# Causal attention whose value products run in two passes instead of three, with the rows' sums taken elementwise

## The chip, the cores and the metric

The kernel runs on one core of one Trainium2 chip. The metric is the device time of one execution in microseconds (us); less is better. The core has a matrix engine (PE, with a separate track PEld for loading the stationary operand), a vector engine (DVE), an activation engine (ACT), a general-purpose engine (POOL) and a queue engine that issues DMA transfers (SP). Each engine runs its own instructions strictly in the order in which they stand in its program, and waits at an instruction until the semaphores that this instruction names have come. PE writes to PSUM only; POOL reads and writes SBUF only.

## The reference, cut to what matters

The whole program is one decoder layer over 2048 tokens of width 1024: an RWKV-7 branch and a latent attention branch on one normalised input, gated and merged, then a mixture of experts. The change lies in the attention branch, 8 heads of 96-wide queries and keys and 64-wide values:

```python
s = (jnp.einsum('bqhd,bkhd->bhqk', q_nope[:, start:end], k_nope[:, :end])
     + jnp.einsum('bqhr,bkr->bhqk', q_rope[:, start:end], k_rope[:, :end]))
s = s.astype(jnp.float32) * scale
causal = jnp.arange(end)[None, :] <= jnp.arange(start, end)[:, None]
p = jax.nn.softmax(jnp.where(causal, s, -jnp.inf), axis=-1).astype(v.dtype)
outs.append(jnp.einsum('bhqk,bkhd->bqhd', p, v[:, :end]))
```

The softmax is done as usual in two steps: the numerator p = exp(s - max), the product of p with the values, and the sum of p over the keys of each query, by which the product is divided later.

## The kernel before, in words

The program goes through phases: input projections (`phase_a`), attention with the RWKV scan beside it (`phase_d`), merge, output projection and router (`phase_f`), experts (`phase_g`), final norm (`phase_z`). All matrix operands of `phase_d` that need accuracy are split into a high part, rounded to the matrix engine's fast 32-bit format (`F32R`), and a low part, the rest. `split` does this: ACT copies the high part (L143), and another engine, for attention POOL, subtracts it from the source for the low part (L144).

`phase_d` works through 32 units, one for each head `h` and each block `qb` of 512 queries. A unit has `4*qb + 4` steps, one for each tile of 128 keys (`kt`); the last four lie on the diagonal and are 512, 384, 256 and 128 queries wide. Over all units that makes 320 steps, 224 of them 512 wide and 32 of each narrower width. In `pass2` a step does this:

- PE makes the scores of 128 keys by up to 512 queries, keys on partitions, in three products (L1044 to L1046) and on the diagonal a fourth that adds the mask (L1048), into a PSUM tile `st` (2 buffers).
- ACT takes the exponential to SBUF, `pf` (L1052, 3 buffers), and copies its high part `ph` (L143). POOL subtracts for the low part `pl` (L144). These have 4 buffers each.
- Three steps later (`flush`), PE multiplies with the values. The value tile `av` holds for each key 192 columns: 64 of the values' low part, 64 of their high part and 64 ones. L1031 multiplies `ph` with [high, ones] (128 columns), L1032 multiplies `ph` with the low part into the same 64 rows of PSUM, and L1036 (for one step in each unit L1061, at the end) multiplies `pl` with [high, ones]. So rows 0 to 63 of `pv` collect the product and rows 64 to 127 the sum of p.
- At the end of a unit ACT copies the product `ob` (L1064) and one row of sums `lb` (L1065) to SBUF, and two DMAs store them.

Between the steps `other()` fills in the rest: `pass1` of a later unit, in which PE makes rough scores with queries on partitions (L982, tiles `sh`, 3 buffers), DVE reduces each to its maximum (L985, masked L988), and the negated maxima (L994) go through PE (L998) and ACT (L999) into a 97th row of the queries; and pieces of the RWKV scan (PE products `sx` on lines 852 to 880, DVE steps on lines 858 to 873, later `post`, lines 889 to 925). A scheduler of the framework then sets the final order of each engine's instructions from its own estimate of time and from the priorities of the code, so that instructions of neighbouring steps stand interleaved. Once per head `load_k` splits the next head's keys and values (POOL, `ak` and `av`).

Of the kernel before, what the change touches and what calls it, by code (L numbers as in the profile page):

```python
# [10 lines left out]
F32 = mybir.dt.float32  # L11
F32R = mybir.dt.float32r
# [3 lines left out]
AF = mybir.ActivationFunctionType  # L16
OP = mybir.AluOpType
# [5 lines left out]
NT = S // 128  # L23
# [64 lines left out]
class K:  # L88
# [842 lines left out]
    def d_open(self):  # L931

        self.dst = ExitStack()
        kp = self.kp = self.dst.enter_context(self.tc.tile_pool(name="attnkv", bufs=1, side="right",
                                                                reuse_waits="tile"))
        self.av = [kp.tile([128, NT, 192], F32R, name="av%d" % j) for j in range(2)]
        for t in self.av:
            self.nc.vector.tensor_copy(t[:, :, 128:], self.c["ones"][:, None, :64].to_broadcast([128, NT, 64]))
        self.idr = kp.tile([128, 128], F32R, name="identr")
        self.nc.vector.tensor_copy(self.idr, self.ident)  # L940
        self.cmq = kp.tile([128, 512], F32, name="cmq")
        self.dma(self.cmq, self.I["cmq"])
        self.q0 = self.load_q(0, 0)
        self.kv0 = self.load_k(0)
        self.p0 = self.pass1(kp, "rw", 4, self.kv0[0], self.q0, 0)
# [56 lines left out]
    def phase_d(self):  # L1002
        nc, tc = self.nc, self.tc
        V, A, T = nc.vector, nc.scalar, nc.tensor
        self.Od = [self.dram("Od%d" % q, [4, 128, 512]) for q in range(4)]
        self.Ld = [self.dram("Ld%d" % q, [H, 512]) for q in range(4)]
        with ExitStack() as st:
            st.push(self.dst.pop_all())
            self.psum(st, "d")
            ap = st.enter_context(tc.tile_pool(name="attn", bufs=1, side="right", reuse_waits="tile"))  # L1010
# [12 lines left out]
            def pass2(h, qb, kk, v, qq, other):  # L1023
                pv = self.pst("pv", 2)
                nk = 4 * qb + 4
                todo, keep = [], []

                def flush():
                    kt, j0, ph, pl = todo.pop(0)
                    cs = slice(j0 * 128, 512)  # L1030
                    T.matmul(pv[:, cs], v[:, kt, 64:], ph[:, cs], start=kt == 0, stop=False)  # L1031
                    T.matmul(pv[0:64, cs], v[:, kt, 0:64], ph[:, cs], start=False, stop=False)  # L1032
                    if kt == 4 * qb:
                        keep.append((kt, pl))
                    else:
                        T.matmul(pv[:, cs], v[:, kt, 64:], pl[:, cs], start=False, stop=False)  # L1036

                for kt in range(nk):
                    j0 = max(0, kt - 4 * qb)
                    cs = slice(j0 * 128, 512)  # L1040
                    ks = slice(kt * 128, (kt + 1) * 128)
                    ps = self.pst("st", 2)
                    dg = kt >= 4 * qb
                    T.matmul(ps[:, cs], kk[0][:, ks], qq[0][:, cs], start=True, stop=False)  # L1044
                    T.matmul(ps[:, cs], kk[0][:96, ks], qq[1][:96, cs], start=False, stop=False)
                    T.matmul(ps[:, cs], kk[1][:96, ks], qq[0][:96, cs], start=False, stop=not dg)  # L1046
                    if dg:
                        T.matmul(ps[:, j0 * 128:(j0 + 1) * 128], self.identb, self.cmkb, start=False, stop=True)  # L1048
                    pf = ap.tile([128, 512], F32, name="pf", bufs=3)
                    ph = ap.tile([128, 512], F32R, name="ph", bufs=4)  # L1050
                    pl = ap.tile([128, 512], F32R, name="pl", bufs=1 if kt == 4 * qb else 4, tag="plx" if kt == 4 * qb else "pl")
                    A.activation(pf[:, cs], ps[:, cs], AF.Exp, scale=SCALE)  # L1052
                    self.split(ph[:, cs], pl[:, cs], pf[:, cs], nc.gpsimd)
                    todo.append((kt, j0, ph, pl))
                    if len(todo) > 3:
                        flush()
                    other()
                while todo:
                    flush()
                kt, pl = keep[0]  # L1060
                T.matmul(pv, v[:, kt, 64:], pl, start=False, stop=True)  # L1061
                ob = ap.tile([64, 512], F32, name="ob", bufs=2)
                lb = ap.tile([1, 512], F32, name="lb", bufs=2)
                A.activation(ob, pv[0:64], AF.Copy)  # L1064
                A.activation(lb, pv[64:65], AF.Copy)  # L1065
                self.dma(self.Od[qb][h // 2, 64 * (h % 2):64 * (h % 2) + 64], ob)
                self.dma(self.Ld[qb][h:h + 1], lb)

            units = [(h, qb) for h in range(H) for qb in range(4)]
            steps = [4 * qb + 4 for h, qb in units]  # L1070
# [741 lines left out]
```

## Time and profile before

| | |
|---|---|
| time, median of 3 runs | 2710.17 us (2708.5 to 2712.07) |
| the profiled execution's own time | 2706.18 us |
| its span, first to last instruction | 2704.4 us |
| attention stage (1065 to 1732 us of the span) | 667 us |
| PE busy in the stage | 634.23 us |
| ACT busy in the stage | 462.57 us |
| DVE busy in the stage | 442.38 us |
| POOL busy in the stage | 415.51 us |
| TensorE clock granted, mean over the stage | 0.96 of full speed |

How to read the profile: it is one execution, taken by the hardware profiler. Busy time of an engine is the time in which at least one of its instructions was recorded as running; an instruction that has started and is held up inside the chip counts as busy. Matmuls are pipelined, so that the recorded length of one is longer than its distance to the next. A wait is idle time of an engine, put down to the instruction whose semaphore came last. Times of day are counted from the first instruction. The attention stage is here the stretch from the first value product (at 1066.6 us) to the last one (at 1731.7 us), widened to whole numbers.

### The profile page before, as it was taken

How to read it: one execution, taken by the hardware profiler on the slowest of the kernel's cores; microseconds unless marked ns; L12 is line 12 of the kernel's file. 1: busy time of each engine (PE TensorE's matmuls, PEld its weight loads, DVE VectorE, ACT ScalarE, POOL GpSimd, SP SyncE). 2: the span in 40 equal slices, each digit the busy share in tenths (PEclk: the TensorE clock that was granted, in tenths of full speed). 3: DMA queues.
4: the chain of work that ended last, by engine and by line, in shares of the span. 5: the costliest groups of instructions: out<-in, count | busy, mean ns of one | idle time of the engine just before them, and what ended most of it. 6: DMA issues, size and time to landing. Idle time of an engine off the chain costs nothing. (4 is left out here: it accounts for less than half of the span.)

```text
span 2704.4 us, 42459 instructions
## 1 busy us (share of the span) xinstructions
PE 2493.0 (92%) x14868; PEld 2033.2 (75%) x14868; DVE 1957.0 (72%) x3466; ACT 1424.3 (53%) x2539; POOL 961.8 (36%) x676
## 2 busy tenths in 40 slices
PE   8999999999999998989999999999999878999991
PEld 6777778788787886767777777777888667989880
DVE  8766699777748994676666766666666678888883
ACT  6554243465443423666776767632232246878774
POOL 3111612401112222556665665402012145555540
PEclk9999999999999998999999999999999979999995
DMA  4556444435563435444443441674554377999987
GB/s 147 125 146 172 137 140 134 171 102 133 142 177 105 138 122 173 129 122 133 129 123 95 129 129 41 205 225 137 184 167 148 125 228 235 329 288 318 299 246 264
DMA packets 334443, 452.46 MB, mean 167 GB/s; under 512 B 170320, under 2 KB 216272, under 8 KB 332944
## 3 DMA queue, kind: packets, MB, share of 16 engines
q1 hardware_dynamic: 320656, 416.03, 49.3%
q0 software_dynamic: 13568, 33.67, 5.5%
q8 instruction: 118, 1.93, 0.3%
q14 instruction: 101, 0.83, 0.1%
HBM read 318.06 MB, written 138.33 MB: 169 GB/s over the span
## 5 line engine op out<-in xcount | busy, mean ns | idle before, releaser
L151 PE MATMUL am<-h,aw 128*128 128x512 f32 x1104 | 440.8, 400 | 21.2 <-ACT h L237 8.5
L144 POOL TENSOR_TENSOR pl<-pf,ph 128x512 fp32r<-128x512 f32 (+1 forms) x320 | 372.8, 1181 | 238.5 <-ACT ph L143 163.3
L153 PE MATMUL am<-h,aw 128*128 128x512 f32 x1104 | 437.8, 397 | 11.9 <-POOL aw L144 7.5
L152 PE MATMUL am<-h,aw 128*128 128x512 f32 x1104 | 437.3, 396 | 0.1
L1562 PE MATMUL gg<-hh,gu 128*128 128x256 f32 (+5 forms) x1024 | 271.0, 338 | 5.4 <-DVE hh L144 5.0
L151 PEld LDWEIGHTS am<-h,aw 128*128 128x128 f32 x1104 | 210.8, 191 | 70.1 <-ACT h L237 8.5
L153 PEld LDWEIGHTS am<-h,aw 128*128 128x128 f32 x1104 | 210.3, 191 | 60.3 <-POOL aw L144 8.7
L1563 PE MATMUL gg<-hh,gu 128*128 128x128 f32 (+5 forms) x1024 | 249.2, 250 | 0.0
L152 PEld LDWEIGHTS am<-h,aw 128*128 128x128 f32 x1104 | 210.5, 191 | 48.6 <-DVE h L238 2.4
L1052 ACT ACTIVATE pf<-st 128x512 f32<-128x512 f32 (+1 forms) x320 | 167.6, 529 | 119.2 <-PE st L1046 65.2
L1562 PEld LDWEIGHTS gg<-hh,gu 128*128 128x128 f32 x1024 | 195.8, 191 | 13.1 <-DVE hh L144 6.6
L1563 PEld LDWEIGHTS gg<-hh,gu 128*128 128x128 f32 x1024 | 198.6, 194 | 4.5
L143 ACT ACTIVATE ph<-pf 128x512 fp32r<-128x512 f32 (+1 forms) x320 | 176.8, 565 | 6.6
L985 DVE TENSOR_REDUCE mx<-sh 128x1 f32<-128x512 f32 x192 | 128.2, 686 | 66.1 <-PE sh L982 64.9
L144 POOL TENSOR_TENSOR aw<-awr,aw 128x1024 fp32r<-128x1024 f32 (+1 forms) x32 | 89.0, 2782 | 241.2 <-ACT aw L143 231.0
L144 DVE TENSOR_TENSOR gu<-graw,gu 128x1024 fp32r<-128x1024 f32 x128 | 155.0, 1239 | 12.0 <-ACT gu L143 10.3
L143 ACT ACTIVATE gu<-graw 128x1024 fp32r<-128x1024 f32 x128 | 131.1, 1056 | 33.8 <-DMA graw<-in_moe_w_gu 31.4
L801 DVE TENSOR_TENSOR inv<-inv,invt 128x62 f32<-128x62 f32 (+30 forms) x124 | 137.9, 1112 | 2.8
L144 POOL TENSOR_TENSOR sum<-sq,sum 128x512 fp32r<-128x512 f32 x16 | 23.5, 1469 | 317.1 <-ACT sum L143 301.3
L799 DVE TENSOR_TENSOR invt<-inv 128x62 f32<-128x62 f32 (+30 forms) x124 | 133.5, 1076 | 2.6
L1044 PE MATMUL st<-aq,ak 97*128 97x512 f32 (+1 forms) x320 | 127.5, 398 | 8.0 <-ACT pf L1052 7.1
L1580 POOL DMA_INDIRECT x2d<-yo,ix x50 | 93.0, 1860 | 104.2 <-DMA x2d<-yo,ix 21.5
(414 smaller groups left out, 6342.8 us busy)
## 6 DMA issues: line engine op xcount, KB each, us to landing
graw<-in_moe_w_gu SPq DMA_DIRECT2D x128, 512.0 KB
awr<-in_w_cols SPq DMA_DIRECT2D x70, 512.0 KB
draw<-in_moe_w_down SPq DMA_DIRECT2D x62, 512.0 KB
gate<-gsb SPq DMA_DIRECT2D x64, 256.0 KB
SC<-SCd SPq DMA_DIRECT2D x32, 512.0 KB
wbr<-in_w_b SPq DMA_DIRECT2D x32, 512.0 KB
gt<-gate SPq DMA_DIRECT2D x32, 512.0 KB
xs<-in_xT SPq DMA_DIRECT2D x32, 256.0 KB
```

Source lines behind the costliest of these rows:

```text
L143: nc.scalar.activation(hi, src, AF.Copy)
L144: (eng or nc.vector).tensor_tensor(out=lo, in0=src, in1=hi.bitcast(F32), op=OP.subtract)
L151: nc.tensor.matmul(ps, lh, rh, start=first and i == 0, stop=False)
L152: nc.tensor.matmul(ps, lh, rl, start=False, stop=False)
L153: nc.tensor.matmul(ps, ll, rh, start=False, stop=last and i == n - 1)
L799: V.tensor_tensor(out=tv, in0=m[:, 0:t, t:t + 1].to_broadcast([128, t, n]), in1=m[:, t:t + 1, t + 1:].to_broadcast([128, t, n]), op=OP.mult)
L801: V.tensor_tensor(out=m[:, 0:t, t + 1:], in0=m[:, 0:t, t + 1:], in1=tv, op=OP.add)
L985: V.reduce_max(mx[:, j, kb:kb + 1], ps[:, :n], axis=AX)
L1044: T.matmul(ps[:, cs], kk[0][:, ks], qq[0][:, cs], start=True, stop=False)
L1052: A.activation(pf[:, cs], ps[:, cs], AF.Exp, scale=SCALE)
L1562: T.matmul(*a, start=k == 0, stop=False)
L1563: T.matmul(*b, start=False, stop=k == 7)
```

## The change: what it does

The value tile loses its ones and holds [low, high], 128 columns for each key, so that one product of `ph` and one of `pl` with this tile give both parts: rows 0 to 63 of `pv` collect p times the low part, rows 64 to 127 p times the high part. L1032 is gone. At the end of a unit ACT copies rows 64 to 127 to `ob`, and DVE adds rows 0 to 63 to it.

The sum of p is now taken in two stages. In each unit a tile `la` (128 keys by 512 queries, 2 buffers) collects the `pf` of all steps by one elementwise addition for each step after the first. Each addition reads `la` and the step's `pf`, both in SBUF, and writes `la` back. Every fourth step (`kt % 4 == 3`) it is issued on POOL, otherwise on DVE. At the end of the unit PE sums `la` over the 128 partitions in two products with ones (plain 32-bit floats, 64 columns of ones by 256 queries each) into a tile `sh`, and ACT copies this to `lb`, from which two rows of 256 are stored. `pf` has 4 buffers instead of 3, since it is now also held until its addition.

```diff
-        self.av = [kp.tile([128, NT, 192], F32R, name="av%d" % j) for j in range(2)]
-        for t in self.av:
-            self.nc.vector.tensor_copy(t[:, :, 128:], self.c["ones"][:, None, :64].to_broadcast([128, NT, 64]))
+        self.av = [kp.tile([128, NT, 128], F32R, name="av%d" % j) for j in range(2)]
...
                 def flush():
                     kt, j0, ph, pl = todo.pop(0)
                     cs = slice(j0 * 128, 512)
-                    T.matmul(pv[:, cs], v[:, kt, 64:], ph[:, cs], start=kt == 0, stop=False)
-                    T.matmul(pv[0:64, cs], v[:, kt, 0:64], ph[:, cs], start=False, stop=False)
+                    T.matmul(pv[:, cs], v[:, kt], ph[:, cs], start=kt == 0, stop=False)
                     if kt == 4 * qb:
                         keep.append((kt, pl))
                     else:
-                        T.matmul(pv[:, cs], v[:, kt, 64:], pl[:, cs], start=False, stop=False)
+                        T.matmul(pv[:, cs], v[:, kt], pl[:, cs], start=False, stop=False)
...
-                    pf = ap.tile([128, 512], F32, name="pf", bufs=3)
+                    pf = ap.tile([128, 512], F32, name="pf", bufs=4)
...
                     self.split(ph[:, cs], pl[:, cs], pf[:, cs], nc.gpsimd)
+
+                    if kt == 0:
+                        la = pf
+                    else:
+                        if kt == 1:
+                            pf0, la = la, ap.tile([128, 512], F32, name="la", bufs=2)
+                            if j0:
+                                V.tensor_copy(la[:, :128], pf0[:, :128])
+                        (nc.gpsimd if kt % 4 == 3 else V).tensor_tensor(
+                            out=la[:, cs], in0=(pf0 if kt == 1 else la)[:, cs], in1=pf[:, cs], op=OP.add)
                     todo.append((kt, j0, ph, pl))
...
-                T.matmul(pv, v[:, kt, 64:], pl, start=False, stop=True)
+                T.matmul(pv, v[:, kt], pl, start=False, stop=True)
+
+                ps = self.pst("sh", 3)
+                for a in range(2):
+                    T.matmul(ps[64 * a:64 * a + 64, :256], self.c["ones"][:, :64], la[:, 256 * a:256 * a + 256],
+                             start=True, stop=True)
                 ob = ap.tile([64, 512], F32, name="ob", bufs=2)
-                lb = ap.tile([1, 512], F32, name="lb", bufs=2)
-                A.activation(ob, pv[0:64], AF.Copy)
-                A.activation(lb, pv[64:65], AF.Copy)
+                lb = ap.tile([128, 256], F32, name="lb", bufs=2)
+                A.activation(ob, pv[64:128], AF.Copy)
+                V.tensor_tensor(out=ob, in0=pv[0:64], in1=ob, op=OP.add)
+                A.activation(lb, ps[:, :256], AF.Copy)
                 self.dma(self.Od[qb][h // 2, 64 * (h % 2):64 * (h % 2) + 64], ob)
-                self.dma(self.Ld[qb][h:h + 1], lb)
+                self.dma(self.Ld[qb][h].rearrange("(a b) -> a b", a=2), lb[0:128:64])
```

Of the 288 additions, DVE has 208 (144 of them 512 wide, 32 each of 384 and 256) and POOL 80 (48 of 512, 32 of 128). DVE also gets 8 copies of 128 columns and 32 additions for `ob`. PE gets 64 products with ones for the 320 that it loses.

The rows below show how the final order of an engine moves. A row gives the line, the operation, what it writes and reads, and its shape; in square brackets stand the engines (PE, Activation for ACT, Pool, DVE) or DMA queues whose semaphore it waits for. Lines of the changed kernel differ by their number: L983 and L986 are the former L985 and L988.

On DVE, in the last block of queries of the fifth head (a unit of 16 steps), the stretch in which pass 1 of a later unit has begun. Before, `mx` and `junk` are the reductions of pass 1, `SV` and `ZV` steps of the scan:

```order
L985 TENSOR_REDUCE mx_14924<-sh_14925 128x1 [waits PE_49]
L988 ISA junk_14957,mx_14924<-sh_14955,cmq_9092 128x128 [waits PE_49]
L988 ISA mx_14924 128x1
L865 TENSOR_TENSOR SV_13917<-sx_14191,isT_105 64x256 [waits DMAHW7_49,PE_49]
L865 TENSOR_TENSOR SV_13917<-sx_14191,isT_105 64x256
L985 TENSOR_REDUCE mx_14924<-sh_15000 128x1 [waits PE_49]
L988 ISA junk_15018,mx_14924<-sh_15016,cmq_9092 128x256 [waits DVE_49,PE_49]
L988 ISA mx_14924 128x1
L985 TENSOR_REDUCE mx_14924<-sh_15045 128x1 [waits PE_49]
```

The same stretch in the changed kernel:

```order
L1059 TENSOR_TENSOR la_14864<-la_14864,pf_14930 128x512 [waits Activation_49,Pool_49]
L894 TENSOR_REDUCE yst_13342<-ysq_14851 128x8 [waits Activation_49]
L983 TENSOR_REDUCE mx_15006<-sh_15007 128x1 [waits PE_49]
L986 ISA junk_15039,mx_15006<-sh_15037,cmq_9090 128x128 [waits PE_49]
L986 ISA mx_15006 128x1
L1059 TENSOR_TENSOR la_14864<-la_14864,pf_14943 128x512 [waits DVE_49,Activation_49]
L983 TENSOR_REDUCE mx_15006<-sh_15082 128x1 [waits PE_49]
L986 ISA junk_15100,mx_15006<-sh_15098,cmq_9090 128x256 [waits DVE_49,PE_49]
L986 ISA mx_15006 128x1
L1059 TENSOR_TENSOR la_14864<-la_14864,pf_14969 128x512 [waits DVE_49,Activation_49]
L983 TENSOR_REDUCE mx_15006<-sh_15127 128x1 [waits PE_49]
```

An addition to `la` now stands ahead of almost every reduction of pass 1, and waits for ACT; the first one shown follows a step whose addition is on POOL, and waits for POOL too.

On POOL, the end of the same unit and the begin of the next one (four steps of 512, 384, 256 and 128). Before:

```order
L144 TENSOR_TENSOR pl_15038<-pf_15036,ph_15037 128x512 [waits Activation_49]
L144 TENSOR_TENSOR pl_15066<-pf_15064,ph_15065 128x384 [waits PE_49,Activation_49]
L144 TENSOR_TENSOR pl_15080<-pf_15078,ph_15079 128x256 [waits PE_49,Activation_49]
L144 TENSOR_TENSOR pl_15118<-pf_15116,ph_15117 128x128 [waits PE_49,Activation_49]
L144 TENSOR_TENSOR pl_15187<-pf_15185,ph_15186 128x512 [waits PE_49,Activation_49,Pool_49]
```

The same place in the changed kernel:

```order
L144 TENSOR_TENSOR pl_15120<-pf_15118,ph_15119 128x512 [waits Activation_49]
L1059 TENSOR_TENSOR la_14864<-la_14864,pf_15089 128x512 [waits DVE_49]
L144 TENSOR_TENSOR pl_15148<-pf_15146,ph_15147 128x384 [waits Activation_49]
L144 TENSOR_TENSOR pl_15162<-pf_15160,ph_15161 128x256 [waits PE_49,Activation_49]
L144 TENSOR_TENSOR pl_15200<-pf_15198,ph_15199 128x128 [waits Activation_49]
L1059 TENSOR_TENSOR la_14864<-la_14864,pf_15198 128x128 [waits DVE_49]
L144 TENSOR_TENSOR pl_15285<-pf_15283,ph_15284 128x384 [waits PE_49,Activation_49]
```

POOL's additions stand between its subtractions and wait for DVE, and the subtractions behind them wait with them.

On PE, the end of the same unit. Before:

```order
L1031 MATMUL pv_14753<-ph_15117,av0_9086 128x128 [waits Activation_49]
L1032 MATMUL pv_14753<-ph_15117,av0_9086 64x128
L1044 MATMUL st_15195<-aq0_14393,ak0_14400 128x384
L1045 MATMUL st_15195<-aq1_14394,ak0_14400 128x384
L1046 MATMUL st_15195<-aq0_14393,ak1_14401 128x384
```

The same place in the changed kernel:

```order
L1029 MATMUL pv_14832<-ph_15199,av0_9086 128x128
L1072 MATMUL sh_15244<-la_14864,cst_116 64x256 [waits DVE_49]
L980 MATMUL sh_15274<-ak0_14475,aq0_14828 128x512
L1033 MATMUL pv_14832<-pl_15200,av0_9086 128x128 [waits Pool_49]
L1068 MATMUL pv_14832<-pl_15120,av0_9086 128x512
```

The second product of each step (L1032) is gone, and the products with ones (L1072, one for each half of the queries) stand among the last value products of the unit; the first half waits for DVE's last addition to it.

## Rows read from the trace of the kernel before

**Rows 1.** The page's first part: busy time, share of the span, instructions

```profile
PE 2493.0 (92%) x14868; PEld 2033.2 (75%) x14868; DVE 1957.0 (72%) x3466; ACT 1424.3 (53%) x2539; POOL 961.8 (36%) x676
```

**Rows 2.** By window: length, PE, PEld, DVE, ACT, POOL busy, clock, DMA, GB/s

```profile
1065.00:1732.00 667.00, 634.23 (x5089) 482.85 (x5088) 442.38 (x877) 462.57 (x870) 415.51 (x334) 0.96 0.43 120
1465.50:1497.00 31.50, 31.50 (x284) 23.60 (x284) 17.57 (x38) 22.05 (x43) 18.82 (x16) 1.00 0.33 95
```

**Rows 3.** Waits in the attention stage: total us, times, longest

```profile
POOL pl L144 <- ACT ph L143: 163.3, 124, 9.3
DVE mx L985 <- PE sh L982: 64.9, 54, 3.6
PE sh L998 <- DVE mr L994: 12.2, 4, 4.2
```

**Rows 4.** Timeline of PE: start us, length us, instruction

```profile
1484.71 0.39 PE L1031 MATMUL pv<-ph,av 128*128 128x512 f32 x1
1484.93 0.39 PE L1032 MATMUL pv<-ph,av 128*64 128x512 f32 x1
1485.17 0.39 PE L1036 MATMUL pv<-pl,av 128*128 128x512 f32 x1
```

**Rows 5.** By line in the stage: count, busy us, mean ns, idle before

```profile
L1032 PE MATMUL pv<-ph,av 128*64 128x512 f32 x224 | 90.6, 404 | 0.0
```

**Rows 6.** Timeline of PE, a product with ones in phase_a

```profile
28.90 1.02 PE L214 MATMUL rw<-xacc,cst 128*128 128x512 f32 x2
```

**Rows 7.** One line of DVE outside attention: min/median/max ns

```profile
L1221 DVE TENSOR_TENSOR gt<-gt x32: 680/691/711, 1743.7 to 2098.4; 128x512 f32<-128x512 f32 x32
```

**Rows 8.** By line in the stage, two DVE shapes

```profile
L988 DVE CUSTOM_DVE_ANT_0 junk<-sh,cmq 128x384 f32<-128x384 f32 x31 | 17.1, 551 | 13.2 <-PE sh L982 12.7
L988 DVE CUSTOM_DVE_ANT_0 junk<-sh,cmq 128x256 f32<-128x256 f32 x31 | 13.0, 419 | 3.1 <-PE sh L982 1.9 <-PE pv L1061 0.5
```

**Rows 9.** Timeline of DVE: two reductions in a row

```profile
1254.82 1.28 DVE L985 TENSOR_REDUCE mx<-sh 128x1 f32<-128x512 f32 x2
```

**Rows 10.** By line in the stage: scan steps, SBUF with SBUF, PSUM with SBUF

```profile
L858 DVE TENSOR_TENSOR zd<-ZV,Dt 64x256 f32<-64x256 f32 x62 | 42.6, 687 | 1.3
L865 DVE TENSOR_TENSOR SV<-sx,isT 64x256 f32<-64x256 f32 x64 | 26.9, 420 | 40.0 <-PE sx L863 39.2
```

**Rows 11.** Timeline of DVE around a POOL subtraction

```profile
1222.86 0.69 DVE L925 TENSOR_TENSOR pgw<-pgw,pq 128x512 f32<-128x512 f32 x1
...
1366.28 1.80 DVE L925 TENSOR_TENSOR pgw<-pgw,pq 128x512 f32<-128x512 f32 x1
```

**Rows 12.** Timeline of POOL: the same places, and three subtractions alone

```profile
1223.04 1.67 POOL L144 TENSOR_TENSOR pl<-pf,ph 128x512 fp32r<-128x512 f32 x1 [0.48 <-ACT ph L143]
...
1257.54 3.70 POOL L144 TENSOR_TENSOR pl<-pf,ph 128x512 fp32r<-128x512 f32 x3
...
1366.24 4.31 POOL L144 TENSOR_TENSOR pl<-pf,ph 128x512 fp32r<-128x512 f32 x3 [1.12 <-ACT ph L143]
```

**Rows 13.** All POOL subtractions for low parts: min/median/max ns

```profile
L144 POOL TENSOR_TENSOR pl<-pf,ph x320: 454/1282/3222, 1066.4 to 1731.1; 128x512 fp32r<-128x512 f32 x127, 128x256 fp32r<-128x256 f32 x32, 128x384 fp32r<-128x384 f32 x1
```

**Rows 14.** By line in the stage: small steps on DVE

```profile
L994 DVE TENSOR_SCALAR mr<-m 128x4 fp32r<-128x4 f32 x31 | 20.2, 653 | 0.9
L890 DVE TENSOR_SCALAR yst<-yst 128x8 f32<-128x8 f32 x16 | 16.4, 1026 | 0.5
```

**Rows 15.** One line of DVE: min/median/max ns

```profile
L994 DVE TENSOR_SCALAR mr<-m x32: 157/226/5522, 1060.1 to 1703.4; 128x4 fp32r<-128x4 f32 x32
```

**Rows 16.** By line in the stage: POOL's subtractions, widest and narrowest

```profile
L144 POOL TENSOR_TENSOR pl<-pf,ph 128x512 fp32r<-128x512 f32 x224 | 293.8, 1326 | 182.9 <-ACT ph L143 115.4 <-PE pv L1032 25.5 <-PE pv L1061 14.8
L144 POOL TENSOR_TENSOR pl<-pf,ph 128x128 fp32r<-128x128 f32 x32 | 19.0, 595 | 20.8 <-ACT ph L143 19.5 <-PE st L1046 1.4
```

More of the change, by code (lines that the diff above doesn't have):

```diff
@@ L1025, in pass2 @@
                 nk = 4 * qb + 4
-                todo, keep = [], []
+                todo, keep, la = [], [], None
                 def flush():
```

## The prediction

> **What bounds the kernel now.** I read the first part of the page, then the attention stage by window, its waits, and the groups by line. PE is the busiest engine of the whole span at 92% [rows 1], and in the attention stage, the only one that the change touches, it is busy 634 of 667 us, ACT 463, DVE 442, POOL 416 [rows 2]. The waits agree: DVE's reductions wait 65 us for the rough scores, and POOL waits 163 us for ACT's high parts; PE's own longest wait is 12 us for a small step of DVE [rows 3]. In a unit of 16 steps PE is never idle, while DVE is busy 17.6 of 31.5 us and POOL 18.8 [rows 2]. So work taken from PE shortens the stage until DVE or POOL, which get the new work, come up to it. What follows the stage begins with products of PE; I let a change of its length pass to the end one to one.
>
> **What PE loses and gains.** Products of 512 columns start 0.22 to 0.24 us apart [rows 4]; I take 0.23, not the recorded 0.40. The removed product is not hidden: nothing runs beside it on PE, and it has no idle time before it [rows 5]. 224 of them by 0.23 are 51.5 us; 32 each of 384, 256 and 128 columns, by their columns, 11.0; together 62.5. The products with ones are plain floats, which the trace runs as two instructions: for 512 columns the pair takes 1.02 us, less the 0.16 us tail by which a recorded product (0.39) outlasts its pace (0.23), so 0.86 [rows 6]. A unit has 512 such columns: 32 x 0.86 = 27.5 us. PE nets 35 us less: 599 us.
>
> **What DVE gains.** Of its 208 additions, 144 are 512 wide, 32 of 384, 32 of 256. One of 512 takes 0.69 us [rows 7], the narrower ones 0.55 and 0.42 by DVE's masked reductions of the same widths [rows 8]. In a row, two take 1.28 together [rows 9], so each moves the queue on by 0.09 less: 0.60, 0.46, 0.33. That is 86 + 15 + 11 = 112 us. The 32 additions for `ob` at 0.60 are 19, the 8 copies 2. Sum: 133 us.
>
> **What the shared way to SBUF costs.** The scan has two DVE steps of the same shape. The one that reads PSUM and SBUF takes 420 ns, the one whose two inputs both lie in SBUF 687 ns [rows 10]: 0.27 us more each. The timeline shows why. An addition that began 0.04 us after a POOL subtraction took 1.80 us instead of 0.69 [rows 11, 12]; and where the addition was first, the subtraction that began 0.18 us later took 1.67, against 1.23 for each of three alone [rows 11, 12]. So each waits for the other. All 208 new additions and the copies read SBUF alone. At the scan step's 0.27 us, raised with POOL's share (416 us plus 48 additions at 1.28 and 32 narrow ones at 0.45, the median and the least of its subtractions [rows 13], which have the same two inputs, is 492 of 667, or 0.74, against 0.62; I use 0.70 for a longer stage, so 0.30 us), 216 of them wait 65 us. The bounds: nothing, if they always find the way free, and 1.11 us each (the addition above), 240 us; I take the scan step because it meets the same subtractions 62 times. The older victims wait more as well: the scan step 62 x 0.27 = 17 us, and the small steps L994 and L890 [rows 14], which take 0.16 us alone [rows 15] and 20.2 and 16.4 us in total, some 29 us of it waiting; 46 us by 0.70/0.62 is 6 more.
>
> A rule speaks against the change here. The Trainium skill, "SBUF — State Buffer", section "Who interferes with whom", says that a DVE instruction with two SBUF inputs and a GpSimd instruction that reads SBUF exclude each other for the whole instruction. The trace agrees in kind; in price it differs, since the subtraction above lost 0.44 us to an addition of 0.69. What full blocking would do at chance arrival is a rival below.
>
> **The sum.** DVE: 442 + 133 + 65 + 6 = 646 us in a stage that now takes 667, more than PE's 599. POOL: 492 plus 0.44 us for each 512 queries of additions (184 such, if all collide: 81) is at most 573. ACT loses and gains under 10 us and stays near 460. DVE becomes the fullest engine. PE reached 95% of the stage as its bound (634/667). DVE will reach less, I take 93%, because it stands in the middle: its reductions wait for PE, its additions for ACT, and every fourth one waits for POOL, whose own additions wait for DVE and hold up the subtractions behind them, which PE's low-part products need. 646/0.93 = 695 us, 28 longer than now. The profiled execution took 2706 us, 4 less than the median of the runs, so 2734 by its own time and 2738 by the runs'.
>
> What is queued behind the new waits: behind an addition on DVE stand the reductions (PE waits for their tiles, 3 buffers), then L994, for which PE already waits; behind POOL's additions stand the subtractions. `pf` is freed later, and its fourth buffer covers one step of that, some 2 us. The products with ones wait for the last additions, but stand among other products; I cost that wait at nothing, and at 0.5 us a unit, 16 us, if nothing covers it. The new DMAs are as many as before and end nowhere near the critical path.
>
> **Rivals.**
> *PE stays the bound.* An addition needs only `pf`, which is there one ACT copy before POOL can begin its subtraction. If DVE is prompt, the additions fall into the time in which POOL waits for ACT [rows 3], hardly collide, and DVE has about 580 us to do. Then the stage loses PE's 35 us: 2671, or 2675 by the runs; with half of the gain eaten by waits 2692. For it: POOL's 163 us of waiting, and the four `pf` buffers. Against: DVE is in order, and reductions that wait for PE stand between the additions.
> *Additions collide at chance.* POOL is busy 0.70 of the time with pieces of 1.28 us, so an arrival at chance waits 0.70 x 0.64 = 0.45 us: 97 us instead of 65, DVE 678, the stage 729: 2768, or 2772 by the runs. This is what the rule of the Trainium skill cited above would give. Against it stands the scan step's 0.27 us at 0.62, under the 0.40 that the same reckoning would give it.
> *DVE and POOL in lockstep.* 48 wide additions on POOL have a next addition on DVE that can't start before them. If each holds DVE for the subtraction ahead and the addition (2.5 us) and nothing useful is lost but half, 48 x 1.25 = 60 us come on top: about 2798. For it: the rows of the order in which POOL waits for DVE; against it, that the scheduler has put other work between.
> *Nothing to measure.* DVE is packed like PE, 646/0.97 = 666 us: 2710. Less than 0.2%, about 5 us, can't be told from no change.
>
> **How the numbers follow.** My forecast (DVE bound, 2738, own range 2718 to 2760) gets 0.44, collision at chance 0.12, lockstep 0.05, PE bound 0.30, nothing to measure 0.09. The first three are slower by over 0.2%: 0.61. The range 2678 to 2778 leaves out the lower half of the PE case, where the full gain is kept, and the lockstep, together near 0.2; it takes in the additions' waits from 30 to 100 us.
>
> **What would show it.** In the stage of the changed kernel: DVE busy near 646 us and over 90%, PE near 600 and under 90%; additions to `la` on DVE of 512 with a mean near 1.0 us instead of 0.69; subtractions on POOL over the 1326 ns of now [rows 16]; waits of DVE for PE's rough scores nearly gone, and PE waiting for DVE's maxima, L994's successor and `pf`. If instead the additions' mean is under 0.8 us and PE still fills 95% of a shorter stage, the prediction is wrong, and the additions did fit beside POOL's waiting.

## Result and the profile after

The changed kernel takes 2823.81 us in the median (2811.15 to 2824.09) against 2709.34 before: ratio 1.0411, 95% interval 1.0386 to 1.0436. The forecast was 2738 with a range up to 2778: slower was right, the size was not.

The profiled execution, at 2811.15 us the shortest of the four, has a span of 2809.0 us, 104.6 longer than before. All of it is in the attention stage: 775.3 us where it was 667 [rows 2]; outside it the two traces agree within some 5 us. The stage by window: length, then busy time (instructions) of PE, PE's weight loads, DVE, ACT and POOL, PE's granted clock, DMA share, GB/s.

```profile
1063.30:1838.60 775.30, 675.64 (x4886) 484.28 (x4886) 662.30 (x1120) 457.25 (x867) 545.49 (x414) 0.88 0.36 103
```

DVE is at 662 us (442 before), POOL at 545 (416); the prediction had 646 and at most 573. But DVE is only 85% of the stage, and no engine fills it. PE is busy longer (676 against 634) with less to do, and its clock was granted at 0.88 instead of 0.96. An estimate from these rows splits the stage: busy time by clock is what PE's work would take at 2.4 GHz, 609 us before and 595 after; the rest of its busy time, 25 and 81, is what 1.2 GHz costs; its idle time is 33 and 100. So 14 us of work went, 56 came by the clock and 67 by idling. The split is rough, since the mean clock counts idle time too.

The groups of the stage by form (busy us, mean ns | idle before, with what ended it):

```profile
L144 POOL TENSOR_TENSOR pl<-pf,ph 128x512 fp32r<-128x512 f32 x224 | 331.2, 1498 | 141.8 <-ACT ph L143 103.4 <-PE pv L1068 18.2 <-DVE mx L986 7.7
L1059 DVE TENSOR_TENSOR la<-la,pf 128x512 f32<-128x512 f32 x120 | 137.5, 1145 | 23.6 <-POOL la L1059 15.8 <-ACT pf L1049 5.5 <-DVE la L1059 0.5
L1059 DVE TENSOR_TENSOR la<-pf 128x512 f32<-128x512 f32 x24 | 34.4, 1431 | 5.1 <-ACT pf L1049 4.7
L1059 POOL TENSOR_TENSOR la<-la,pf 128x512 f32<-128x512 f32 x48 | 64.7, 1348 | 30.1 <-DVE la L1059 12.8 <-ACT pf L1049 6.8 <-ACT ph L143 3.8
L1072 PE MATMUL sh<-la,cst 128*64 128x256 f32 x128 | 43.6, 490 | 5.2 <-DVE la L1059 5.1
```

The additions take 1.145 us, the first of a unit 1.431, instead of the 0.69 of [rows 7]; the subtractions 1498 ns instead of the 1326 of [rows 16]. The waits have turned round:

```profile
POOL pl L144 <- ACT ph L143: 121.7, 53, 10.3
POOL la L1059 <- DVE la L1059: 40.4, 28, 5.6
PE sh L996 <- DVE mr L992: 25.5, 18, 4.1
DVE mx L983 <- PE sh L980: 25.4, 22, 4.0
PE sh L980 <- DVE mx L983: 18.6, 17, 6.9
PE sh L980 <- DVE mx L986: 9.8, 8, 2.2
PE pv L1033 <- POOL pl L144: 10.9, 19, 1.7
```

DVE's wait for rough scores (the `mx` line) fell from 65 us to 25. PE now waits 28 us for DVE's maxima (L983 and L986), and for L992 (the L994 of before) 25 us instead of the 12 of [rows 3]: 54 of its 100 us of idle time. Before, its waits for maxima were these, and with those for L994 16 of 33 us:

```profile
PE sh L982 <- DVE mx L985: 3.8, 3, 3.3
```

What such a wait does, in the timeline of DVE (start, us, engine, line):

```profile
1373.43 3.66 DVE L890 TENSOR_SCALAR yst<-yst 128x8 f32<-128x8 f32 x1
1377.13 5.23 DVE L891 TENSOR_TENSOR yq<-yq,yst 128x512 f32<-128x512 f32 x1
1382.28 1.28 DVE L983 TENSOR_REDUCE mx<-sh 128x1 f32<-128x512 f32 x2
```

and in three windows around it:

```profile
1369.20:1376.10 6.90, 6.90 (x43) 4.72 (x43) 6.31 (x9) 4.65 (x7) 4.28 (x3) 1.00 1.12 298
1376.10:1383.00 6.90, 0.00 (x0) 0.00 (x0) 6.87 (x4) 2.18 (x3) 5.71 (x4) 0.68 0.45 90
1383.00:1392.20 9.20, 8.45 (x22) 5.89 (x23) 7.50 (x15) 6.92 (x12) 5.06 (x4) 0.50 0.09 19
```

Two DVE steps stand 8.9 us, in which POOL has four instructions back to back; the maxima behind them are late; PE, full until 1376.1, does nothing for 6.9 us; and then it works for 9.2 us at a clock of 0.50, its lower level of 1.2 GHz. One late maximum is paid twice. The place shows how a late maximum is paid, and not that the additions made it late: neither of the two DVE steps, nor any of the four POOL instructions, is an addition to `la`. Such meetings are in the trace of before too (L890 took 16.4 us in all there [rows 14], and 14.5 here), but there PE stopped 3.3 us at most for a maximum.

### The profile page after: what moved, and what is told of

It reads as the page before. It is cut to its first block, busy times and chain, and to the rows that moved or that the text cites. A ratio compares the mean times of both kernels' runs of the same rounds, so it can differ in the third digit from the quotient of the medians.

```text
span 2809.0 us, 42605 instructions
## 1 busy us (share of the span) xinstructions
PE 2537.6 (90%) x14676; PEld 2036.5 (72%) x14676; DVE 2176.8 (77%) x3712; ACT 1419.0 (51%) x2539; POOL 1098.1 (39%) x756
## 5 line engine op out<-in xcount | busy, mean ns | idle before, releaser
L144 POOL TENSOR_TENSOR pl<-pf,ph 128x512 fp32r<-128x512 f32 (+1 forms) x320 | 421.2, 1337 | 160.9 <-ACT ph L143 121.7
L1059 DVE TENSOR_TENSOR la<-la,pf 128x512 f32<-128x512 f32 (+2 forms) x176 | 176.5, 1003 | 26.1 <-POOL la L1059 15.8
L980 PE MATMUL sh<-ak,aq 96*128 96x512 f32 (+2 forms) x316 | 125.9, 434 | 29.5 <-DVE mx L983 18.6
L983 DVE TENSOR_REDUCE mx<-sh 128x1 f32<-128x512 f32 x192 | 128.2, 682 | 28.2 <-PE sh L980 26.9
L1041 PE MATMUL st<-aq,ak 97*128 97x512 f32 (+1 forms) x320 | 137.2, 429 | 5.3 <-ACT pf L1049 3.3
```

Source lines behind the costliest of these rows:

```text
L144: (eng or nc.vector).tensor_tensor(out=lo, in0=src, in1=hi.bitcast(F32), op=OP.subtract)
L983: V.reduce_max(mx[:, j, kb:kb + 1], ps[:, :n], axis=AX)
L1059: (nc.gpsimd if kt % 4 == 3 else V).tensor_tensor(out=la[:, cs], in0=(pf0 if kt == 1 else la)[:, cs], in1=pf[:, cs], op=OP.add)
```

## Experiments

Each kernel is compared with the kernel before on its own chip. The stage's figures come from the window row of each.

| kernel | us | ratio (95%) | stage | PE busy | clock | DVE | POOL |
|---|---|---|---|---|---|---|---|
| before | 2709 | 1 | 667 | 634 | 0.96 | 442 | 416 |
| changed | 2824 | 1.0411 (1.0386-1.0436) | 775 | 676 | 0.88 | 662 | 545 |
| no additions | 2693 | 0.9941 (0.9920-0.9962) | 650 | 605 | 0.94 | 459 | 419 |
| reductions for additions | 2739 | 1.0114 (1.0087-1.0141) | 692 | 626 | 0.91 | 585 | 486 |
| scratch additions | 2810 | 1.0382 (1.0353-1.0411) | 763 | 660 | 0.87 | 678 | 535 |
| all additions on DVE | 2860 | 1.0569 (1.0542-1.0596) | 797 | 690 | 0.86 | 700 | 466 |
| third product back | 2802 | 1.0333 (1.0304-1.0362) | 768 | 697 | 0.94 | 664 | 554 |
| reductions of a constant | 2763 | 1.0207 (1.0176-1.0238) | 707 | 630 | 0.91 | 586 | 489 |
| all additions on POOL | 2929 | 1.0818 (1.0787-1.0849) | 892 | 762 | 0.79 | 552 | 731 |
| sums by 64 columns of ones | 2810 | 1.0382 (1.0349-1.0414) | 760 | 728 | 0.93 | 434 | 413 |
| ones in one low column | 2673 | 0.9852 (0.9833-0.9870) | 632 | 586 | 0.93 | 459 | 423 |
| changed, copy | 2808 | 1.0366 (1.0340-1.0393) | 764 | 687 | 0.89 | 563 | 325 |
| no additions, copy | 2697 | 0.9966 (0.9943-0.9990) | 650 | 613 | 0.93 | 422 | 233 |
| scratch additions, copy | 2748 | 1.0149 (1.0105-1.0192) | 705 | 636 | 0.93 | 564 | 322 |
| changed, copy, constant sums | 2769 | 1.0228 (1.0207-1.0249) | 740 | 658 | 0.90 | 573 | 330 |
| changed, copy, all on DVE | 2755 | 1.0191 (1.0160-1.0222) | 711 | 654 | 0.89 | 585 | 260 |

**No additions.** The two products stay; the products with ones read a constant tile `lac`.

```
-                    if kt == 0:
...
-                            out=la[:, cs], in0=(pf0 if kt == 1 else la)[:, cs], in1=pf[:, cs], op=OP.add)
-    T.matmul(ps[64 * a:64 * a + 64, :256], self.c["ones"][:, :64], la[:, 256 * a:256 * a + 256],
+    T.matmul(ps[64 * a:64 * a + 64, :256], self.c["ones"][:, :64], self.lac[:, 256 * a:256 * a + 256],
```

> The changed kernel without its 288 additions to la; the products with ones stay and read a constant tile that makes every row's sum 1, so the output's sums are left out. Every theory: PE has the 35 us less that the prediction gave it and DVE and POOL have nothing new but the 32 additions for ob, so the stage falls from 775.6 us to some 630 to 645 us and the time to 2672 to 2690 us, below the kernel before. If instead it stays above 2710 us, the PE saving itself is false and the additions are not what costs.

Measured 2693, just above the expectation: the two passes together with the products with ones are worth 16 us, and the additions, with all that hangs on them, cost 131.

**Reductions for additions, and scratch additions.** In the first, DVE reads each `pf` with one input and POOL adds `pf` to itself; in the second, both add `pf` to itself into a scratch tile of their own. Neither hands a sum on; `lac` as above.

```
+                        V.reduce_max(ld[:, 0:1], pf[:, cs], axis=AX)
```
```
+                        lp = ap.tile([128, 512], F32, name="lp" if kt % 4 == 3 else "ld")
...
+                            out=lp[:, cs], in0=pf[:, cs], in1=pf[:, cs], op=OP.add)
```

> As e1_noadd, but each addition on DVE is replaced by a reduction of pf to its maximum: one SBUF input, same width, as long on DVE (0.69 us for 512) as an addition that meets nobody. POOL keeps its 80 additions, of pf with itself into a scratch tile, so nothing passes between DVE and POOL. Sums left out. Theory of the shared way to SBUF (additions and subtractions keep each other out): no collisions, DVE has about 580 us to do, the stage falls to 640 to 680 us, the time to 2680 to 2720 us. Theory of DVE's plain time (133 us more on an engine in order is too much, whatever it meets): the stage stays over 730 us, the time over 2775 us. Theory of the handing over of la between DVE and POOL: also recovered, 2700 to 2740 us.

> As e1_noadd, but all 288 additions run on the engines of the changed kernel, each of pf with itself into a scratch tile of its engine: two SBUF inputs as in the changed kernel, but no addition waits for one of the other engine. Sums left out. Theory of the shared way: collisions stay, the time stays at 2790 to 2825 us. Theory of the handing over: the chain is gone, the time falls to 2710 to 2750 us.

2739 and 2810. The first is above what the shared way gave (to 2720), far below DVE's plain time, and only in the range of the handing over; the second is in the range of the shared way alone. The same number of DVE instructions, with POOL's 80 additions in both, costs 46 us with one input from SBUF, and 71 more with two. In the second the means are high:

```profile
L1056 DVE TENSOR_TENSOR ld<-pf 128x512 f32<-128x512 f32 x144 | 191.1, 1327 | 12.2 <-ACT pf L1051 10.1
L144 POOL TENSOR_TENSOR pl<-pf,ph 128x512 fp32r<-128x512 f32 x224 | 329.7, 1489 | 171.9 <-ACT ph L143 132.4 <-PE sh L982 16.6 <-PE pv L1035 7.3
```

From here to the changed kernel only 14 us are left. I first read that as the price of handing the sum over; the runs with the copy, below, show that it isn't the whole of it.

**All additions on DVE, all on POOL.**

```
-                        (nc.gpsimd if kt % 4 == 3 else V).tensor_tensor(
+                        V.tensor_tensor(
```

> The changed kernel with all 288 additions on DVE; output as the reference's. DVE gets 48 x 0.60 + 32 x 0.2 = 35 us more, POOL 76 us less, and nothing is handed over any more. Theory of the shared way: about as many pairs meet, each once per step; DVE's waits change little, the time is 2800 to 2850 us. Theory of the handing over: the time falls below 2780 us. Theory of DVE's plain time: 35 us more and a fuller engine, 2855 us or more.

> The changed kernel with every addition (and the copy) on GpSimd: no addition of VectorE's is left to collide with GpSimd's subtractions, and nothing is handed from engine to engine. GpSimd's work in the stage, 419 us without additions, becomes 419 plus 192 additions of 512 columns at its 1.35 us and 96 shorter ones, some 760 to 780 us. Shared way: VectorE's other two-input work is small, so the collisions (71 us) go, and GpSimd itself becomes the bound: stage 770 to 830 us, 2815 to 2880 us. VectorE's load alone sets the time (the rival): without it the stage falls back to some 700 us, 2745 us.

2860 and 2929 (for the latter, `nc.gpsimd` in both places). Neither engine can take them alone. The first is above the range of the shared way (to 2850) and in that of DVE's plain time; but plain time gave 2775 or more for the reductions, which took 2739, and with the copy below the same additions on DVE take 2755. On POOL the expectation was too low: the collisions did not go, they moved. POOL is busy 731 of the stage's 892 us, and DVE's old steps stand beside it:

```profile
L858 DVE TENSOR_TENSOR zd<-ZV,Dt 64x256 f32<-64x256 f32 x62 | 72.4, 1168 | 1.4
L992 DVE TENSOR_SCALAR mr<-m 128x4 fp32r<-128x4 f32 x31 | 33.0, 1065 | 0.8
```

against 687 and 653 ns in [rows 10, 14]; the clock falls to 0.79.

**The third product put back.**

```
+                    T.matmul(pv[0:64, cs], v[:, kt, 0:64], ph[:, cs], start=False, stop=False)
```

> The changed kernel, with the low values' product that it took out put back (its result is thus added twice into the output: 224 products of 512 columns and the shorter ones more, with nothing else changed). Shared way sets the stage (775.6 us after, TensorE busy 675.9, granted clock 0.88): TensorE has 100 us of idle time in the stage, the product is ready when its neighbour is, and busier it may be granted a higher clock; the 60 us of added product time cost 0 to 20 us, so 2824 to 2845 us. TensorE sets the stage (the rival): the product costs what it cost before, 35 to 62 us, so 2860 to 2885 us.

With 320 products more it is faster, which neither expectation had: 2802, where the interval of its ratio (to 1.0362) ends below that of the changed kernel (from 1.0386). PE's clock by fortieths of the span, of the changed kernel and of this one:

```profile
PEclk9999999999999998788899898899999979999996
```
```profile
PEclk9999999999999999999999999999999979999996
```

The row of dips in the stage is gone, and PE's idle time is 71 us instead of 100. So TensorE's work does not set the changed kernel's time: the product that the change removed costs nothing there.

**Reductions of a constant.**

```
-                        V.reduce_max(ld[:, 0:1], pf[:, cs], axis=AX)
+                        V.reduce_max(ld[:, 0:1], self.lac[:, cs], axis=AX)
```

> As the run with one-input reductions in place of VectorE's additions (2739 us, stage 691.6), but the reductions read a constant tile and not the exponentials, so none waits for ScalarE in VectorE's order and none holds an exponentials' buffer; GpSimd's additions of a tile with itself stay; the row sums are products with a constant tile. If VectorE's plain time is what the additions cost beside the collisions: same as that run within 8 us, 2731 to 2747 us. If it was the wait for the exponentials in VectorE's order (the rival): back towards the run without additions (2693), 2700 to 2720 us.

2763 is outside both expectations: slower by 24 us than the reductions of `pf`, with DVE equally busy (586 and 585 us). DVE's waits for `pf` are thus not what those cost; why the freer order is slower stays open.

**The copy, four times.** POOL's two-input subtraction becomes a copy of the high part, which still waits for ACT. Made in the changed kernel, in the one without additions and in the one with scratch additions:

```
-                    self.split(ph[:, cs], pl[:, cs], pf[:, cs], nc.gpsimd)
+                    A.activation(ph[:, cs], pf[:, cs], AF.Copy)
+                    nc.gpsimd.tensor_copy(pl[:, cs], ph[:, cs].bitcast(F32))
```

> The changed kernel with all its additions, but GpSimd's subtraction with two inputs is a copy of the high part with one input (the low part is thus wrong in the result); it still waits for ScalarE as before. Shared way for two inputs in SBUF: the collisions between VectorE's additions and the subtractions go, those with GpSimd's own 80 additions stay; the stage falls from 775 by 40 to 75 us, 2745 to 2785 us, and VectorE's additions fall from 1.145 us to 0.7 to 0.85. The additions' cost is in VectorE and the order alone (the rival), not in meeting GpSimd: 2805 to 2830 us, with additions over 1 us.

> The run without additions (2693 us, stage 649.8), with GpSimd's subtraction replaced by its one-input copy of the high part, as in the run that made the copy in the changed kernel (2808, where VectorE's additions fell to 0.757 us and its busy time to 563 us, yet the stage stayed at 764 with TensorE busy 687): additions and low parts are left out of the result. If the copy itself costs TensorE time (through what the second pass multiplies, or what the faster GpSimd does to it), this is slower than 2693 by 30 us or more. If the copy is harmless and the additions or the handing over of their sum still cost the 764, it is 2680 to 2700 us.

> The run in which each exponential is added to itself into a scratch tile (2810 us, stage 763), with GpSimd's subtraction replaced by its one-input copy: no sum is handed over, the products with ones read a constant tile, and VectorE's two-input additions meet only GpSimd's own 80. If meeting the subtractions is the cost, 2730 to 2755 us. If the handing over of the sum is what kept the changed kernel with the copy at 2808, also 2730 to 2755 us, and then that run's remainder of some 60 us is the handing over. If the copy itself costs TensorE time, 2790 us or more.

In the changed kernel the additions fell to 0.757 us, and the time hardly did (2808):

```profile
L1051 POOL CAST pl<-ph 128x512 fp32r<-128x512 f32 x223 | 155.1, 699 | 238.1 <-ACT ph L1050 140.7 <-PE pv L1033 55.4 <-PE pv L1029 14.8
L1060 DVE TENSOR_TENSOR la<-la,pf 128x512 f32<-128x512 f32 x120 | 90.9, 757 | 22.4 <-ACT pf L1049 13.9 <-POOL la L1060 4.8 <-POOL pl L1051 1.0
```

My expectation of 2745 to 2785 fell; 2808 is in the range of the rival, whose additions over 1 us did not come. The meetings did not go either, they got shorter: an addition that starts just after a copy still waits for it.

```profile
1123.38 0.61 POOL L1051 CAST pl<-ph 128x512 fp32r<-128x512 f32 x1 [0.50 <-ACT ph L1050]
1123.41 1.13 DVE L1060 TENSOR_TENSOR la<-pf 128x512 f32<-128x512 f32 x1
```

The copy is harmless without additions (2697), and with scratch additions it gives 2748, which both of its theories had. So four kernels stand in a square: copy and scratch additions 2748, subtraction and scratch additions 2810, copy and the real sum 2808, subtraction and the real sum 2824. Each of the two steps is worth 60 us without the other, and only 14 or 16 on top of it; these last two are near the noise, as the intervals of the ratios overlap. The subtraction's step is its longer meetings and its load in one, for with scratch additions the copy takes POOL from 535 us to 322. The real sum's step is a chain from addition to addition, over two engines, and products with ones that read its end.

**Which part of the handing over.** In the copy's kernel, the products with ones read `lac`, so PE waits for no sum; or all additions go to DVE, so nothing is handed over.

```
-    T.matmul(ps[64 * a:64 * a + 64, :256], self.c["ones"][:, :64], la[:, 256 * a:256 * a + 256],
+    T.matmul(ps[64 * a:64 * a + 64, :256], self.c["ones"][:, :64], self.lac[:, 256 * a:256 * a + 256],
```
```
-                        (nc.gpsimd if kt % 4 == 3 else V).tensor_tensor(
+                        V.tensor_tensor(
```

> The changed kernel with GpSimd's subtraction as a copy (2808 us), and the products with ones read a constant tile, so TensorE waits for no sum; the sum is still handed from VectorE to GpSimd and back (low parts and the sums are left out of the result). If the handing over between the engines holds the exponentials and with them ScalarE and TensorE, 2795 to 2815 us. If TensorE's wait for the sum in its own order is what costs the 60 us (products with ones stand ahead of the next unit's work), 2740 to 2765 us.

> The changed kernel with GpSimd's subtraction as a copy (2808 us), and all additions on VectorE: nothing is handed over and nothing meets a two-input instruction of GpSimd, but VectorE carries the 80 additions that GpSimd had (48 of 512 columns and 32 of 128, at 0.69 and 0.2 us some 40 us more). The products with ones wait for the sum as in the changed kernel (low parts are left out of the result). If the handing over costs the 60 us: 2745 to 2785 us. If it is TensorE's wait for the sum: 2805 to 2850 us.

2769, 4 us above what the theory of PE's wait gave, and 2755, within that of the handing over. With the constant 39 of the 60 us go, without the handing over 53, although DVE then does POOL's 80 additions too; these two overlap as well, since together they are more than 60. That PE waits for a late sum is not what the traces record: PE's idle time before these products is 1.5 us in the copy's kernel and 5.1 in the changed one. They record another thing, first the sum (L1073), then the constant (L1075), by form and in one unit each:

```profile
L1073 PE MATMUL sh<-la,cst 128*64 128x256 f32 x128 | 45.6, 471 | 1.5 <-DVE la L1060 1.5
L1075 PE MATMUL sh<-lac,cst 128*64 128x256 f32 x128 | 26.5, 463 | 2.9 <-DVE mx L985 2.8
```
```profile
1187.44 0.65 PE L1073 MATMUL sh<-la,cst 128*64 128x256 f32 x2
1193.47 0.65 PE L1073 MATMUL sh<-la,cst 128*64 128x256 f32 x2
```
```profile
1203.60 0.65 PE L1075 MATMUL sh<-lac,cst 128*64 128x256 f32 x4
```

With the sum, the two halves of a unit mostly stand apart in PE's order, and each takes 0.65 us; with the constant they mostly stand together, and both take 0.65 us. So 19 of the 39 us are PE's own time, which the constant saves by the order alone; where the other 20 come from is not shown. With all additions on DVE the halves stand apart too (41.2 us), and 53 of the 60 us go all the same. POOL's 80 additions go there together with the handing over; that they are cheap by themselves, the scratch additions with the copy (2748) show. So what costs is mainly that the sum changes engines; that it comes late by that, and that PE needs it then, is argued and not shown. The 21 us that are left with the constant stand beside these waits of DVE and POOL for each other, and of ACT for a `pf` that an addition still holds:

```profile
POOL la L1062 <- DVE la L1062: 39.3, 30, 3.4
DVE la L1062 <- POOL la L1062: 9.3, 4, 3.5
ACT pf L1051 <- DVE la L1062: 44.8, 40, 4.1
```

**Two other ways to the sums.** First, 64 columns of ones times the high part in a bank taken from the rough scores, with the low-part product in bf16 beside it.

```
+                    T.matmul(pw[0:64, cs], self.onr, ph[:, cs], start=kt == 0, stop=kt == nk - 1, skip_group_check=True)
-                        T.matmul(pv[:, cs], v[:, kt], pl[:, cs], start=False, stop=False)
+                        T.matmul(pv[64:128, cs], vb[:, kt], pl[:, cs], start=False, stop=False, skip_group_check=True)
```

> A candidate: no elementwise additions. The rows' sums are products of 64 columns of ones with the high part of the exponentials alone (their low part's share of the sum is left out), into a bank taken from the score maxima (three of these buffers become two); the low part of the exponentials and the high part of the values for it are bf16, and that product goes to the 64 rows that the ones' product leaves. PE-bound: three products of 512 columns again, so some 0.39 us x 224 more than in the run without additions (2693), 2700 to 2755 us, about the time before. If the two 64-row products run beside each other: 2690 to 2705 us. Shared way: GpSimd's subtraction writes half the bytes, VectorE has no additions: no collisions, so nothing near 2824.

2810: no new DVE load (434 us) and no gain, for now PE fills 96% of the stage, and the narrow product is recorded as long as the removed one was (404 ns [rows 5]). That is above both expectations.

```profile
L1036 PE MATMUL pw<-ph,onr 128*64 128x512 f32 x224 | 90.5, 415 | 0.0
```

Those lengths do not explain why 5080 products fill 760 us here and 5089 filled 667 before. The starts explain most of it: these products follow each other by 0.31 to 0.33 us, at a granted clock of 1.00, where the three of [rows 4] follow by 0.22 to 0.24.

```profile
1500.94 0.47 PE L1035 MATMUL pv<-ph,av 128*128 128x512 f32 x1
1501.25 0.40 PE L1036 MATMUL pw<-ph,onr 128*64 128x512 f32 x1
1501.58 0.40 PE L1040 MATMUL pv<-pl,avb 128*64 128x512 bf16 x1
1501.91 0.50 PE L1035 MATMUL pv<-ph,av 128*128 128x512 f32 x1
```

By an estimate from these rows, 0.1 us on each of three products in 224 steps is 67 of the 93 us. Whether the widths, the number format or the change of bank makes the pace was not tested.

Second, a column of ones in place of one of the 64 low columns, so that the sum is one more row of the products that are there anyway.

```
+            self.nc.vector.tensor_copy(t[:, :, 63:64], self.c["ones"][:, None, :1].to_broadcast([128, NT, 1]))
...
+        nc.gpsimd.tensor_tensor(out=v[:, :, 0:63], in0=vr[:, :, 0:63], in1=v[:, :, 64:127].bitcast(F32), op=OP.subtract)
+                A.activation(lb[32:64], pv[32:64], AF.Copy)
```

> A candidate that keeps the two passes and has no additions: in the two-pass weights one of the 64 low columns of the values (the last of each head) is replaced by ones, so that the rows' sums come out of the same products as one output row; that column's low part is left out of the result. Against the run without additions (2693, stage 649.8) it also drops the products with ones and their buffer of the score maxima. Theory (additions and collisions cost it all, the two passes were worth 16 us): 2670 to 2695 us, stage 628 to 652. TensorE idle and its clock falling (the rival): the 22 us of products that go come back as a lower clock, 2693 to 2709 us.

```profile
1063.50:1695.60 632.10, 586.24 (x4759) 452.32 (x4758) 458.58 (x904) 460.83 (x866) 422.77 (x334) 0.93 0.44 126
```

2672.52 (2667.68 to 2672.84), 1.5% faster than before: the two passes without their price, at that of one low column in 64. PE's work by the estimate above is 545 us, 64 less than before; 37 us of it arrive, the rest goes to a lower clock and to idling.

## Why the prediction was wrong, point by point

*PE's loss.* The removed product was put at 62.5 us, and the kernel with the column of ones, which removes it and adds nothing to PE, shows 64. The net of 35 us after the products with ones holds by the same estimate where these stand ready (569 without additions, 40 less than before), not in the changed kernel (595): there they take 43.6 us of PE, since their halves stand apart, instead of the 25.6 of this row of the kernel without additions. The 27.5 of the forecast fits the second.

```profile
L1065 PE MATMUL sh<-lac,cst 128*64 128x256 f32 x128 | 25.6, 433 | 0.0
```

*DVE's gain and the shared way.* 646 us was forecast, 662 measured; subtractions over 1326 ns and additions near 1.0 us came as said. The additions' excess, 1.145 - 0.69 = 0.455 us, is the 0.45 of the rival that let them collide at chance, not the 0.30 taken. The Trainium skill, "SBUF — State Buffer", section "Who interferes with whom", has the two kinds of instruction shut each other out for a whole instruction; for the additions this trace agrees, at those 0.455 us, while the subtractions' mean grew by only 0.17. That rival's time, 2772, was still 52 us short, as it fills DVE to the same share.

*The step that failed* is "DVE will reach less, I take 93%". It reached 85%: at 93% its 662 us would make a stage of 712, and the stage took 775. The forecast treated DVE as a bound that is filled to some share. The runs show that the share doesn't set the time: DVE's load was no higher in the copy's kernel with the real sum (563 us) than in that with scratch additions (564), and their times differ by 60 us; with products that read a constant in both, it is 573 against 564 us of load, and still 21 us. In place of a filled DVE the changed kernel shows waits: PE stands 54 us for the maxima and L992, 16 before, and its clock is low after such a stop (0.50 in the window above). How much of the 108 us in the stage each of these waits makes stays open. The clock, 56 us of the stage, was in no term of the sum; it is not a cause by itself, for with the third product it was back at 0.94 and the stage only 8 us shorter.

*The products with ones' wait* was costed at nothing, with 16 us as its bound. PE's recorded wait for the sum is 5.1 us in the changed kernel, so this was not far off. What the forecast did not have is that their halves come apart and then take 43.6 us instead of 27.5.

*The rivals.* Lockstep of DVE and POOL was named, with 60 us and a chance of 0.05. The real sum alone does cost 60, but that the numbers agree is luck: 39 of the 60 go when only the products with ones read a constant, and the lockstep's reckoning has nothing of these products; and the costs overlap and don't add. "PE stays the bound" had 0.30; in no run with additions did PE fill the 95% of [rows 2] again, at most 92% (654 of 711, all on DVE with the copy).

## What to carry to other kernels

A product that fills an engine which is full can still be the cheapest place for a sum, and best is a place in a product that runs anyway. Where work moves from the full engine to one on which it waits, ask not how full that one will be but which small result behind the new work the full engine needs next. Two costs measured one at a time, in one order, look like a big and a small one; only all four combinations showed that each was the same size and hid the other. And a run that puts a constant in place of a result takes away more than the wait for it: it also frees the order, so the trace has to show that what it was meant to remove was there.

## What was not expected of the hardware

An instruction of DVE can stand through several of POOL's in a row: an addition took 4.75 us beside these (DVE, then POOL).

```profile
1478.22 4.75 DVE L1059 TENSOR_TENSOR la<-pf 128x512 f32<-128x512 f32 x1
```
```profile
1474.96 4.59 POOL L144 TENSOR_TENSOR ak<-akr,ak 96x2048 fp32r<-96x2048 f32 x1 [0.75 <-ACT ak L143]
1479.50 4.60 POOL L144 TENSOR_TENSOR pl<-pf,ph 128x128 fp32r<-128x128 f32 x4
```

The last row joins four subtractions, one of 128 columns and three of 512.

More work for TensorE made the kernel faster, 2802 against 2824 us, with the granted clock of the stage at 0.94 instead of 0.88. And an addition of DVE waits for a one-input copy of POOL too (1.13 us above). That the additions' mean with the copy, 0.757 us, is close to the 0.69 of one alone goes with copies that are short (0.61 us there) and a POOL that is busy only 325 of 764 us.
